# Half of the third modulation section, summed over its k-tiles by GpSimd during the first stage

## The chip, the core and the metric
One core of a Trainium2 chip runs the kernel. The metric is the device time of one execution in microseconds. Of the core's engines the text names TensorE (PE in the rows; PEld is its weight load), VectorE (DVE), ScalarE (ACT), GpSimd (POOL) and SyncE (SP). SP here only issues DMAs; its queue is "SP's queue".

## What is computed
One layer of a diffusion backbone on 128 context tokens and 256 latent tokens (three token tiles of 128) with D = 2048. What matters here is the modulation:

```python
mod_ctx = (silu(c_ctx) @ w_ada + b_ada)      # 6 * D columns: shift1, scale1, gate1, shift2, scale2, gate2
mod_lat = (silu(c) @ w_ada + b_ada)
h = rmsnorm(x, pre1) * (1.0 + scale1) + shift1
proj = h @ w_in                              # then DeltaNet heads (A), mLSTM heads (B)
x = x + gate1 * rmsnorm(mix @ w_out, post1)
h = rmsnorm(x, pre2) * (1.0 + scale2) + shift2
x = x + gate2 * rmsnorm(relu(h @ w1) ** 2 @ w2, post2)
```

`w_ada` has 2048 rows and 12288 columns of float32, so each of the six sections of 2048 columns is 16.8 MB. There are two condition vectors, one for context and one for latents. "The third modulation section", section 2 in the code, is gate1. It is needed only after the output projection.

## The kernel before
All weights are float32 and stream once from HBM. `gemm` (line 343) takes them in chunks of two k-tiles by 512 columns (512 KB). For each chunk `wchunk` (line 326) issues a load on SP's queue into one of five `raw` buffers, ScalarE casts it to a high part `whi`, VectorE subtracts to get the residual `wlo` (lines 338 and 339, both have two buffers), and TensorE makes three products per k-tile and tile (lines 362 to 368). So the chain load, cast, residual, product stands behind every chunk.

The stages are: stage 1 (`phase1`, line 393), which takes 9 pieces of k-tiles (1, 1, then 2 each) and for every piece runs 6 chunks: two for the mLSTM q and k, two for v, two for the output gate; in the last piece the gate columns follow (`gates`, line 523, a long list of small VectorE and TensorE instructions); then the mLSTM heads (`mlstm_head`, line 630), the DeltaNet quarters (lines 784 to 1057) with their own chunks, the output projection (`mid`, line 1082) and the FFN (line 1144).

The modulation is spread between the chunks. After every chunk `gemm` calls `fill` (line 241), which adds `S.rate` to a credit and takes that many steps from the list `S.todo`. A step is one turn of a generator. There are two kinds:

- `ada_steps` (line 177): TensorE multiplies the condition columns `c.scz` (128 rows, 32 columns of which two are used) with raw w_ada tiles, four column groups of 256 per k-tile side by side in one PSUM bank (line 196). The loads stand on SP's queue and use the same five `raw` buffers. At the end `ada_cols` (line 164) copies, transposes twice and copies back, and `ada_mod` adds the bias.
- `ada_vec` (line 210): VectorE multiplies a raw tile with a condition column and adds it to an accumulator (line 226); after 16 k-tiles TensorE sums over the partitions with a matrix of ones. It idles (yields) while its buffer `S.av` isn't there, which is until the output projection.

In stage 1 the list holds sections 0 and 1 at rate 2.0. After the mLSTM stage `body` (line 1222) appends the rest in this order: section 2 (two units of `ada_steps`, 16 k-tiles each), the gate rows, section 3, section 4, section 5, the last gate rows; rate 1.3 in the DeltaNet stage. `mid` drains the list up to the gate rows of gate1 first.

GpSimd in stage 1 issues a few small loads and selects at the start; later it takes the power in `rstd_of` (line 290), two kinds of small copies in the mLSTM heads (lines 635 and 683), and in the FFN a product (line 1163) and, at the very end, products with the gate rows (line 1183).

Each engine runs its instructions in one fixed order, made when the program is built: program order, but an instruction whose inputs come late may be overtaken by later ones, and parts marked with a high priority come early. Tiles are in pools; a tile with `bufs=1` can be taken again only when all that read the former one are done. When the pool of stage 1 (`S.p1`) closes, the mLSTM heads' tiles take its memory.

Of the kernel before, what the change touches and what calls it, by code (L numbers as in the profile page):

```python
# [12 lines left out]
F32 = mybir.dt.float32  # L13
F32R = mybir.dt.float32r
BF16 = mybir.dt.bfloat16
ALU = mybir.AluOpType
# [5 lines left out]
P = 128  # L22
D = 2048
NK = D // P
# [19 lines left out]

def setup(S):
    nc, tc, A = S.nc, S.tc, S.A
    cp, tp = S.cp, S.tp
    c = S.c = SimpleNamespace()

# [160 lines left out]
def ada_vec(S, sec, c0):  # L210

    nc, c = S.nc, S.c
    while S.av is None:
        yield
    acc = S.av.tile([P, 2, 512], F32, tag="adav", name="adav", bufs=1)
    for kt in range(NK):
        if kt % 2 == 0:
            raw = S.wp.tile([P, 2, 512], F32, tag="raw", name="raw_av", bufs=S.nraw)
            nc.sync.dma_start(raw, S.A.w_ada[0, kt * P:(kt + 2) * P, sec * D + c0:sec * D + c0 + 512]
                              .rearrange("(k p) n -> p k n", p=P))  # L220
        for v in range(2):
            w = c.scz[:, kt, v:v + 1]
            if kt == 0:
                nc.vector.tensor_scalar(acc[:, v, :], raw[:, 0, :], w, None, op0=ALU.mult)
            else:
                nc.vector.scalar_tensor_tensor(acc[:, v, :], in0=raw[:, kt % 2, :], scalar=w, in1=acc[:, v, :],  # L226
                                               op0=ALU.mult, op1=ALU.add)
        if kt % 2:
            yield
    ps = S.pa.tile([P, 512], F32, tag="a", name="ps_av")  # L230
    for j in range(4):
        nc.tensor.matmul(ps[32 * j:32 * j + 32, 0:256], lhsT=c.ones[:, 0:32], rhs=acc[:, j % 2, 256 * (j // 2):][:, 0:256],
                         start=True, stop=True)
    t = ada_cols(S, ps, 256)
    pv = S.wk.tile([P, 4, 2], F32, tag="modsum4", name="modsum4")
    for h in range(2):
        nc.vector.tensor_copy(pv[:, 2 * h:2 * h + 2, :].rearrange("p i v -> p v i"), t[:, 2 * h:2 * h + 2, :, 0])
    ada_mod(S, sec, c0 // P, 4, pv)


def fill(S, n=None):

    if n is None:
        S.credit += S.rate
        n = int(S.credit)
        S.credit -= n
    while n > 0 and S.todo:
        try:
            next(S.todo[0])
            n -= 1  # L250
        except StopIteration:
            S.todo.pop(0)
            n -= 1


def drain(S, left):
# [4 lines left out]
def ada_later(S, sec, nvec=0):  # L261

    for i in range(2):
        if i < 2 - nvec:
            S.todo.append(ada_steps(S, [(sec, 1024 * i + 256 * u) for u in range(4)], 256))
        else:
            S.todo.extend(ada_vec(S, sec, 1024 * i + 512 * h) for h in range(2))
# [75 lines left out]
def gemm(S, fm, wsrc, kcs, act, evac, psum=None, kn=2, between=None, room=()):  # L343

    nc = S.nc
    psum = psum or (lambda s: S.pg.tile([P, 512], F32, tag="g", name="ps_g"))
    ps = [None] * 4
    nl = len(kcs) - len(room)  # L350

    def products(s, i, kc, hi, lo):
        if ps[s] is None:
            ps[s] = psum(s)
        o = ps[s][:, 0:TOK] if fm else ps[s]
        w = slice(s * P, s * P + P)
        for kk in range(kn):
            ah, al = act(kn * kc + kk)
            st = i == 0 and kk == 0
            sp = i == len(kcs) - 1 and kk == kn - 1  # L360
            if fm:
                nc.tensor.matmul(o, lhsT=hi[:, kk, w], rhs=al, start=st, stop=False)  # L362
                nc.tensor.matmul(o, lhsT=hi[:, kk, w], rhs=ah, start=False, stop=False)  # L363
                nc.tensor.matmul(o, lhsT=lo[:, kk, w], rhs=ah, start=False, stop=sp)  # L364
            else:
                nc.tensor.matmul(o, lhsT=al[:, w], rhs=hi[:, kk, :], start=st, stop=False)  # L366
                nc.tensor.matmul(o, lhsT=ah[:, w], rhs=hi[:, kk, :], start=False, stop=False)  # L367
                nc.tensor.matmul(o, lhsT=ah[:, w], rhs=lo[:, kk, :], start=False, stop=sp)  # L368
    held = []
    for i, kc in enumerate(kcs):  # L370
        if between:
            between(i)
        w = wchunk(S, wsrc(kc), kn, room[i - nl] if i >= nl else None)
        ns = w[0].shape[2] // P if fm else NT
        if i >= nl:
            held.append((i, kc, *w))
            continue
        for s in range(ns):
            products(s, i, kc, *w)
            if i == len(kcs) - 1:  # L380
                evac(s, ps[s])
        fill(S)
    for s in range(ns if held else 0):
        for h in held:
            products(s, *h)
        evac(s, ps[s])
# [6 lines left out]
def phase1(S):  # L393

    nc, tc, A, c = S.nc, S.tc, S.A, S.c
# [6 lines left out]
    for t in range(NT):  # L402
        junk = p1.tile([P, D], F32, tag="junk", name="junk", bufs=1)
# [11 lines left out]
    for p, (k0, kn) in enumerate(pieces):  # L415
        if p == 0:
            drain(S, NP - 1)

        def acc(dst, src):
            if p == 0:  # L420
                nc.scalar.copy(dst, src)
            else:
                nc.vector.tensor_tensor(dst, src, dst, op=ALU.add)
        if p == 0:
            build_hT(S, xs, 0, 0, diag)
            for t in range(NT):
                nc.vector.tensor_scalar(xs[t], xs[t], r[:, t:t + 1], None, op0=ALU.mult)
            wgh, wgl = setup3(S, p1)

        def next_hT():  # L430
            if p < NP - 1:
                drain(S, NP - 2 - p)
                k1, n1 = pieces[p + 1]
                for kt in range(k1, k1 + n1):
                    build_hT(S, xs, kt, 0)
        kps = (k0 // kn,)
        ps = S.pm.tile([P, 512], F32, tag="m", name="ps_gates")
        for kk in range(kn):
            ah, al = S.hT(k0 + kk)
            for i, (w, a) in enumerate(((wgh, al), (wgh, ah), (wgl, ah))):  # L440
                nc.tensor.matmul(ps[0:GW, 0:TOK], lhsT=w[:, k0 + kk, :], rhs=a, start=kk == 0 and i == 0,
                                 stop=kk == kn - 1 and i == 2)
        acc(gT[0:GW, :], ps[0:GW, 0:TOK])
        for i, c0 in enumerate((C_BQ, C_BK)):
            gemm(S, True, wcols(w_in, c0, 512, kn), kps, S.hT, lambda s, ps, i=i: acc(S.bqk[s][:, i, :], ps[:, 0:TOK]),
                 kn=kn)
        for n in range(2):
            gemm(S, False, wcols(w_in, C_BV + 512 * n, 512, kn), kps, S.hT,
                 lambda s, ps, n=n: acc(S.vaug[s][:, 2 * n:2 * n + 2, 0:DVB],
                                        ps.rearrange("p (a b) -> p a b", a=2)), kn=kn)  # L450
        if p == NP - 1:
            for t in range(NT):
                nc.vector.memset(S.vaug[t][:, :, DVB:DVB + 1], 1.0)
            with tc.high_priority(HP):
                gates(S, gates_cols(S, gT))

        def bo_evac(s, ps, n):
            acc(bo[n][s], ps)
            if p == NP - 1:
                nc.scalar.activation(bo[n][s], bo[n][s], AF.Sigmoid)  # L460
                nc.sync.dma_start(S.gbd[s][:, n * 512:n * 512 + 512], bo[n][s])
        if p == 1:
            setup2(S)
        for n in range(2):
            if n == 1:
                next_hT()
            gemm(S, False, wcols(w_in, C_BO + 512 * n, 512, kn), kps, S.hT, lambda s, ps, n=n: bo_evac(s, ps, n),
                 kn=kn)
# [753 lines left out]
def body(tc, A, O):  # L1222
    with ExitStack() as ctx:
        nc = tc.nc
        S = SimpleNamespace(nc=nc, tc=tc, A=A, O=O, todo=[], credit=0.0, rate=1.7, nraw=5, av=None)
        ent = ctx.enter_context
        sub = lambda st, nm, bufs=1: st.enter_context(tc.tile_pool(name=nm, bufs=bufs, reuse_waits="tile"))
        S.cp = ent(tc.tile_pool(name="cp", bufs=1))
# [11 lines left out]
        with ExitStack() as mx:  # L1240
# [3 lines left out]
            with ExitStack() as ms:  # L1244
                S.mp = sub(ms, "mp")
                S.ga = sub(ms, "ga")
                with tc.tile_pool(name="p1", bufs=1, reuse_waits="tile") as S.p1:
                    with tc.tile_pool(name="tp", bufs=1, reuse_waits="tile") as S.tp:
                        setup(S)
                    phase1(S)  # L1250
                S.ml = sub(ms, "ml", 2)
                S.n1 = S.ml.tile([P, 8], F32, name="n1", bufs=1)
                for h in range(HB):
                    mlstm_head(S, h)
                mlstm_norms(S)
# [2 lines left out]
            S.de = sub(mx, "de", 2)  # L1258
            S.yA = S.da.tile([P, NT, 1024], F32, name="yA", bufs=1)
            delta_static(S)  # L1260
            ada_later(S, 2)
            S.todo.append(gate_step(S, 0))
            ada_later(S, 3)
            ada_later(S, 4, ND2)
# [43 lines left out]
```

## Time and profile before

| what | us |
|---|---|
| median of 3 runs (1989.87 to 1993.47) | 1989.95 |
| the profiled execution | 1993.48 |
| its span, first to last instruction | 1991.8 |
| TensorE busy | 1944.7 |
| VectorE busy | 1167.4 |
| ScalarE busy | 711.4 |
| GpSimd busy | 127.2 |

Times in the rows count from the start of the span. A group of the view by lines gives line, engine, operation, output and inputs, shapes and count; then the busy time, the mean of one in ns and the idle time before them with what ended it. A row of the timeline gives start, duration, engine, line, operation, tiles, shapes and count, and in brackets how long the engine had been idle and what ended that. "Releaser" and "waited for" are inferred from semaphores.

### The profile page before, as it was taken

The numbers are of one execution on the slowest core, as the hardware profiler recorded it, in microseconds if no ns is written. First come the engines' busy times: TensorE is split into PE (matmuls) and PEld (weight loads), VectorE is DVE, ScalarE is ACT, GpSimd is POOL, SyncE is SP. The second block draws the span as 40 slices with busy tenths as digits, with TensorE's granted clock in tenths as the row PEclk, the third lists the DMA queues.
The fourth block names the chain that finished last, engine by engine and source line by source line (L and its number), as shares of the span: only waits on it lengthen the run. The fifth ranks groups of instructions, "written<-read, shape, count | busy, mean of one in ns | idle before, by whom it ended". The sixth has DMA issues, their size and how long they took to land.

```text
span 1991.8 us, 28827 instructions
## 1 busy us (share of the span) xinstructions
PE 1944.7 (98%) x11334; PEld 1674.3 (84%) x11334; DVE 1167.4 (59%) x2146; ACT 711.4 (36%) x1125; POOL 127.2 (6%) x138
## 2 busy tenths in 40 slices
PE   6999999999999999998999999999999999999997
PEld 4777888888887777788998998988989989989886
DVE  3766885677877756767554565556543443343445
ACT  5222244644345324335433342332332423323322
POOL 3000000100000000000100010000000100000002
PEclk9999999999999999998999999999999999999999
DMA  8988436576656567762455555545544444444453
GB/s 274 299 263 267 124 113 213 177 219 167 184 168 174 167 183 222 265 190 75 148 159 158 169 159 155 161 154 165 158 138 127 127 128 127 129 130 126 133 170 106
DMA packets 229908, 337.25 MB, mean 169 GB/s; under 512 B 43808, under 2 KB 113136, under 8 KB 228748
## 3 DMA queue, kind: packets, MB, share of 16 engines
q1 hardware_dynamic: 211640, 333.14, 54.2%
q10 hardware_dynamic: 17620, 2.11, 0.7%
q8 instruction: 89, 1.46, 0.3%
q14 instruction: 47, 0.39, 0.1%
q0 software_dynamic: 512, 0.15, 0.1%
HBM read 326.80 MB, written 8.56 MB: 168 GB/s over the span
## 4 chain that ended last, share of the span: by engine, by line
PE 90%; DVE 4%; DMA 4%; ACT 1%; SPq 1%; issue 1%; POOL 0%; DVEq 0%; POOLq 0%; ACTq 0%
PE ps_g L362 13%; PE ps_g L364 12%; PE ps_g L363 12%; PE ps_dn L366 9%; PE ps_dn L368 8%; PE ps_dn L367 8%; PE ps_g L366 5%; PE ps_g L368 5%; PE ps_g L367 5%; PE ps_ada L196 4%; DMA raw<-w_in 2%; DVE wlo L339 1%; PE ps_num L694 1%; PE ps_o L1042 1%; PE ps_z L1008 1%
## 5 line engine op out<-in xcount | busy, mean ns | idle before, releaser
L339 DVE TENSOR_TENSOR wlo<-raw,whi 128x1024 fp32r<-128x1024 f32 (+1 forms) x402 | 487.5, 1213 | 558.0 <-ACT whi L338 556.9
L338 ACT CAST whi<-raw 128x1024 fp32r<-128x1024 f32 (+1 forms) x402 | 417.6, 1039 | 998.7 <-PE ps_g L363 386.8
L362 PE MATMUL ps_g<-h,whi 128*128 128x384 f32 x1536 | 522.7, 340 | 0.5 <-DVE cv L752 0.5
L364 PE MATMUL ps_g<-h,wlo 128*128 128x384 f32 x1536 | 516.5, 337 | 3.3 <-DVE wlo L339 3.3
L363 PE MATMUL ps_g<-h,whi 128*128 128x384 f32 x1536 | 516.7, 336 | 0.1
L362 PEld LDWEIGHTS ps_g<-h,whi 128*128 128x128 f32 x1536 | 288.9, 188 | 20.8 <-issue 18.4
L368 PE MATMUL ps_dn<-wlo,ah 128*128 128x512 f32 x756 | 294.5, 390 | 1.2 <-DVE wlo L339 1.2
L366 PE MATMUL ps_dn<-whi,al 128*128 128x512 f32 x756 | 294.9, 390 | 0.0
L367 PE MATMUL ps_dn<-whi,ah 128*128 128x512 f32 x756 | 294.5, 390 | 0.0
L364 PEld LDWEIGHTS ps_g<-h,wlo 128*128 128x128 f32 x1536 | 288.6, 188 | 6.6 <-DVE wlo L339 5.5
L363 PEld LDWEIGHTS ps_g<-h,whi 128*128 128x128 f32 x1536 | 289.0, 188 | 1.1 <-issue 0.7
L368 PEld LDWEIGHTS ps_dn<-wlo,ah 128*128 128x128 f32 x756 | 141.9, 188 | 31.6 <-DVE wlo L339 2.1
L366 PEld LDWEIGHTS ps_dn<-whi,al 128*128 128x128 f32 x756 | 141.9, 188 | 31.0 <-issue 1.6
L367 PEld LDWEIGHTS ps_dn<-whi,ah 128*128 128x128 f32 x756 | 141.9, 188 | 28.8
L226 DVE SCALAR_TENSOR_TENSOR adav<-raw_av,scz,adav 128x512 f32<-128x512 f32 x180 | 130.6, 774 | 13.2 <-DMA raw_av<-w_ada 13.1
L1163 POOL TENSOR_TENSOR rl<-rl 128x384 f32<-128x384 f32 x64 | 68.1, 1072 | 876.0 <-ACT ah L1162 875.9
L366 PE MATMUL ps_g<-whi,h 128*128 128x512 f32 x288 | 119.4, 415 | 0.6 <-ACT whi L338 0.6
L367 PE MATMUL ps_g<-whi,h 128*128 128x512 f32 x288 | 116.0, 403 | 0.0
L368 PE MATMUL ps_g<-wlo,h 128*128 128x512 f32 x288 | 114.4, 401 | 0.5 <-DVE wlo L339 0.5
L196 PE MATMUL ps_ada<-raw_ada,scz 128*32 128x256 f32 (+1 forms) x1216 | 101.7, 389 | 4.0 <-DMA raw_ada<-w_ada 2.6
L366 PEld LDWEIGHTS ps_g<-whi,h 128*128 128x128 f32 x288 | 54.8, 190 | 23.5 <-issue 11.5
L368 PE MATMUL ps_g<-wlo,y 128*128 128x512 f32 x180 | 71.1, 395 | 1.5 <-DVE wlo L339 1.5
(409 smaller groups left out, 1862.3 us busy)
## 6 DMA issues: line engine op xcount, KB each, us to landing
raw<-w_ffn SPq DMA_DIRECT2D x256, 512.0 KB, 3.8
raw_ada<-w_ada SPq DMA_DIRECT2D x80, 512.0 KB, 4.0
raw<-w_in SPq DMA_DIRECT2D x74, 512.0 KB, 4.0
raw_ada<-w_ada SPq DMA_DIRECT2D x128, 256.0 KB, 4.5
raw_av<-w_ada SPq DMA_DIRECT2D x48, 512.0 KB, 4.4
raw<-w_in SPq DMA_DIRECT2D x76, 256.0 KB, 3.9
raw<-w_out SPq DMA_DIRECT2D x32, 512.0 KB, 4.6
x<-x_sample SPq DMA_DIRECT2D x2, 1024.0 KB, 9.8
```

What stands on the lines that cost most here:

```text
L196: nc.tensor.matmul(ps[32 * j:32 * j + 32, 0:n], lhsT=c.scz[:, k + kk, :], rhs=raw[:, kk, u * n:u * n + n], start=k + kk < npar, stop=k + k ...
L226: nc.vector.scalar_tensor_tensor(acc[:, v, :], in0=raw[:, kt % 2, :], scalar=w, in1=acc[:, v, :], op0=ALU.mult, op1=ALU.add)
L338: nc.scalar.copy(hi, raw)
L339: nc.vector.tensor_tensor(lo, raw, hi.bitcast(F32), op=ALU.subtract)
L362: nc.tensor.matmul(o, lhsT=hi[:, kk, w], rhs=al, start=st, stop=False)
L363: nc.tensor.matmul(o, lhsT=hi[:, kk, w], rhs=ah, start=False, stop=False)
L364: nc.tensor.matmul(o, lhsT=lo[:, kk, w], rhs=ah, start=False, stop=sp)
L366: nc.tensor.matmul(o, lhsT=al[:, w], rhs=hi[:, kk, :], start=st, stop=False)
L367: nc.tensor.matmul(o, lhsT=ah[:, w], rhs=hi[:, kk, :], start=False, stop=False)
L368: nc.tensor.matmul(o, lhsT=ah[:, w], rhs=lo[:, kk, :], start=False, stop=sp)
L694: nc.tensor.matmul(o, lhsT=l, rhs=r, start=n == 0, stop=n == len(ops) - 1)
L1163: nc.gpsimd.tensor_tensor(rl, rl, rl, op=ALU.mult)
```

## The change
Columns 1024 to 2047 of section 2 leave the list after the mLSTM stage. Instead, from the third piece of stage 1 on, a second list `S.ptodo` holds two `ada_pool` generators for 512 columns each, called half 0 and half 1 in the text. Per step one pair of k-tiles is loaded by a DMA issued from GpSimd, one pair ahead, into a double buffer that takes the memory of an earlier scratch tile; GpSimd multiplies the raw tile with the condition column into `tmpp` and adds that to the accumulator `adap`, for each of the two conditions. `fill_pool` takes half a step per chunk. After 8 steps and two empty ones `ada_sum`, the tail of `ada_vec` made a function, sums over the partitions on TensorE and goes on as before. `adap`, the double buffer and `tmpp` have one buffer each. Steps left when stage 1 ends are taken right there.

```diff
--- before.py
+++ after.py
@@ -227,6 +227,43 @@
                                                op0=ALU.mult, op1=ALU.add)
         if kt % 2:
             yield
+    ada_sum(S, sec, c0, acc)
+
+
+def ada_pool(S, sec, c0):
+
+    nc, c = S.nc, S.c
+    acc = S.mp.tile([P, 2, 512], F32, tag="adap", name="adap", bufs=1)
+    both = S.p1.tile([P, 2, 2, 512], F32, tag="junk", name="rawp", bufs=1)
+
+    def load(kt):
+        raw = both[:, kt // 2 % 2]
+        nc.gpsimd.dma_start(raw, S.A.w_ada[0, kt * P:(kt + 2) * P, sec * D + c0:sec * D + c0 + 512]
+                            .rearrange("(k p) n -> p k n", p=P))
+        return raw
+    ahead = load(0)
+    for kt in range(0, NK, 2):
+        raw = ahead
+        if kt + 2 < NK:
+            ahead = load(kt + 2)
+        for kk in range(2):
+            for v in range(2):
+                w = c.scz[:, kt + kk, v:v + 1]
+                if kt + kk == 0:
+                    nc.gpsimd.tensor_scalar(acc[:, v, :], raw[:, 0, :], w, None, op0=ALU.mult)
+                else:
+                    tmp = S.p1.tile([P, 512], F32, tag="tmpp", name="tmpp", bufs=1)
+                    nc.gpsimd.tensor_scalar(tmp, raw[:, kk, :], w, None, op0=ALU.mult)
+                    nc.gpsimd.tensor_tensor(acc[:, v, :], acc[:, v, :], tmp, op=ALU.add)
+        yield
+    for _ in range(2):
+        yield
+    ada_sum(S, sec, c0, acc)
+
+
+def ada_sum(S, sec, c0, acc):
+
+    nc, c = S.nc, S.c
     ps = S.pa.tile([P, 512], F32, tag="a", name="ps_av")
     for j in range(4):
         nc.tensor.matmul(ps[32 * j:32 * j + 32, 0:256], lhsT=c.ones[:, 0:32], rhs=acc[:, j % 2, 256 * (j // 2):][:, 0:256],
@@ -251,6 +288,16 @@
         except StopIteration:
             S.todo.pop(0)
             n -= 1
+
+
+def fill_pool(S):
+    S.pcredit += S.prate
+    while S.pcredit >= 1 and S.ptodo:
+        S.pcredit -= 1
+        try:
+            next(S.ptodo[0])
+        except StopIteration:
+            S.ptodo.pop(0)
 
 
 def drain(S, left):
@@ -380,6 +427,7 @@
             if i == len(kcs) - 1:
                 evac(s, ps[s])
         fill(S)
+        fill_pool(S)
     for s in range(ns if held else 0):
         for h in held:
             products(s, *h)
@@ -461,6 +509,9 @@
                 nc.sync.dma_start(S.gbd[s][:, n * 512:n * 512 + 512], bo[n][s])
         if p == 1:
             setup2(S)
+        if p == 2:
+            S.ptodo = [ada_pool(S, 2, 1024 + 512 * h) for h in range(2)]
+            S.prate = 0.5
         for n in range(2):
             if n == 1:
                 next_hT()
@@ -1222,7 +1273,7 @@
 def body(tc, A, O):
     with ExitStack() as ctx:
         nc = tc.nc
-        S = SimpleNamespace(nc=nc, tc=tc, A=A, O=O, todo=[], credit=0.0, rate=1.7, nraw=5, av=None)
+        S = SimpleNamespace(nc=nc, tc=tc, A=A, O=O, todo=[], credit=0.0, rate=1.7, nraw=5, av=None, pcredit=0.0, prate=0.0, ptodo=[])
         ent = ctx.enter_context
         sub = lambda st, nm, bufs=1: st.enter_context(tc.tile_pool(name=nm, bufs=bufs, reuse_waits="tile"))
         S.cp = ent(tc.tile_pool(name="cp", bufs=1))
@@ -1248,6 +1299,9 @@
                     with tc.tile_pool(name="tp", bufs=1, reuse_waits="tile") as S.tp:
                         setup(S)
                     phase1(S)
+                while S.ptodo:
+                    S.prate = 1.0
+                    fill_pool(S)
                 S.ml = sub(ms, "ml", 2)
                 S.n1 = S.ml.tile([P, 8], F32, name="n1", bufs=1)
                 for h in range(HB):
@@ -1258,7 +1312,7 @@
             S.de = sub(mx, "de", 2)
             S.yA = S.da.tile([P, NT, 1024], F32, name="yA", bufs=1)
             delta_static(S)
-            ada_later(S, 2)
+            S.todo.append(ada_steps(S, [(2, 256 * u) for u in range(4)], 256))
             S.todo.append(gate_step(S, 0))
             ada_later(S, 3)
             ada_later(S, 4, ND2)
```

## Rows read from the trace of the kernel before
**Rows 1.** The page: head, GpSimd's busy tenths in 40 slices, chain of waits by engine.
```profile
span 1991.8 us, 28827 instructions
...
POOL 3000000100000000000100010000000100000002
...
PE 90%; DVE 4%; DMA 4%; ACT 1%; SPq 1%; issue 1%; POOL 0%; DVEq 0%; POOLq 0%; ACTq 0%
```

**Rows 2.** Busy times of stretches of stage 1; columns in the first row.
```profile
core 0: us, PE busy (x) PEld busy (x) DVE busy (x) ACT busy (x) POOL busy (x), PEclk, DMA share, GB/s
...
40.00:80.00 40.00, 39.43 (x277) 26.02 (x279) 27.13 (x61) 14.97 (x26) 0.00 (x0) 1.00 0.97 315
80.00:120.00 40.00, 39.93 (x271) 29.98 (x270) 25.62 (x41) 8.09 (x9) 0.00 (x0) 1.00 0.84 263
...
200.00:260.00 60.00, 60.00 (x301) 52.80 (x300) 50.36 (x78) 17.73 (x20) 0.31 (x2) 1.00 0.43 124
260.00:300.00 40.00, 39.67 (x205) 33.53 (x204) 30.65 (x87) 17.75 (x25) 0.00 (x0) 0.96 0.36 111
```

**Rows 3.** Waits, 25 to 200 us: total, times, longest.
```profile
ACT whi L338 <- DMA raw<-w_in: 67.8, 21, 5.9
```

**Rows 4.** Timeline at 118 us: start, us, engine, line, out<-in, count [idle before].
```profile
118.04 1.04 ACT L338 CAST whi<-raw 128x1024 fp32r<-128x1024 f32 x1 [5.33 <-DMA raw<-w_in]
...
120.40 0.50 PE L368 MATMUL ps_g<-wlo,h 128*128 128x512 f32 x1 [0.47 <-DVE wlo L339]
```

**Rows 5.** Timeline at 221 us: VectorE, then TensorE.
```profile
220.74 1.23 DVE L339 TENSOR_TENSOR wlo<-raw,whi 128x1024 fp32r<-128x1024 f32 x1 [0.17 <-ACT whi L338]
...
224.22 0.39 PE L368 MATMUL ps_g<-wlo,h 128*128 128x512 f32 x1
```

**Rows 6.** Groups by line, TensorE, 300 to 800 us.
```profile
L196 PE MATMUL ps_ada<-raw_ada,scz 128*32 128x256 f32 x638 | 59.7, 389 | 0.0
```

**Rows 7.** Timeline at 409 us, TensorE.
```profile
409.19 1.07 PE L196 MATMUL ps_ada<-raw_ada,scz 128*32 128x256 f32 x16
```

**Rows 8.** Line 1183 on GpSimd: min/median/max in ns.
```profile
L1183 POOL TENSOR_TENSOR y<-y,gp x9: 1288/1298/2280, 1931.6 to 1966.7; 128x512 f32<-128x512 f32 x9
```

**Rows 9.** Groups by line and shape, GpSimd, whole span.
```profile
L129 POOL DMA_DIRECT2D gbias<-mlstm_ibias x1 | 1.5, 1504 | 0.0
L764 POOL MEMSET Tm<- 128x768 f32 x2 | 1.4, 741 | 0.0
```

**Rows 10.** Timeline at 1965 us, VectorE.
```profile
1964.75 0.69 DVE L1177 TENSOR_TENSOR y<-ps_dn,y 128x512 f32<-128x512 f32 x1 [0.67 <-PE ps_dn L368]
1965.82 2.01 DVE L339 TENSOR_TENSOR wlo<-raw,whi 128x1024 fp32r<-128x1024 f32 x1 [0.38 <-ACT whi L338]
```

**Rows 11.** Timeline of the same stretch, GpSimd.
```profile
1964.19 4.78 POOL L1183 TENSOR_TENSOR y<-y,gp 128x512 f32<-128x512 f32 x3 [11.55 <-ACT fj L1180]
```

**Rows 12.** Chain of waits in order of time, 200 to 260 us.
```profile
201.57 0.66 PE ps_hT L303 x6
...
228.01 0.66 PE ps_hT L303 x6
```

**Rows 13.** Timeline, VectorE, the gate columns: first, one between, last.
```profile
263.90 0.20 DVE L531 TENSOR_TENSOR gz<-gt,gbias 128x48 f32<-128x48 f32 x1
...
270.19 0.20 DVE L555 SCALAR_TENSOR_TENSOR gg<-gl,gea 128x48 f32<-128x48 f32 x1
...
295.25 0.17 DVE L511 TENSOR_TENSOR r3r<-r3r,nmrp 128x24 f32<-128x24 f32 x1
```

**Rows 14.** Timeline at 270 us, TensorE.
```profile
270.90 1.40 PE L564 MATMUL ps_cum<-gg,tri 128*128 128x8 f32 x12
```

**Rows 15.** Chain of waits in order of time, 255 to 312 us: stage 1's last product.
```profile
294.37 0.23 PE ps_g L368
```

**Rows 16.** Timeline, GpSimd, 255 to 312 us.
```profile
254.94 0.31 POOL L635 COPY cn<-n 128x2 f32<-128x2 f32 x2 [233.26 <-PE ps_hT L303]
311.35 0.19 POOL L683 COPY n<-cf 128x1 f32<-128x1 f32 x1 [56.10 <-ACT cf L681]
```

## The prediction
> **What bounds the kernel now.** I read the page's chain of waits first: 90% of the span is TensorE work [rows 1], so a microsecond counts where TensorE has to wait or is spared instructions. Next the busy times by stretch of stage 1, where the change puts its work [rows 2]. Three regimes are to be seen. From 40 to 80 us the DMA engines are 0.97 busy at 315 GB/s. From 80 to 120 us they are 0.84 busy at 263 and TensorE is full. From 200 to 260 us, the first two modulation sections being through, DMA moves 124 GB/s and TensorE alone sets the pace. Then ScalarE's wait list: the cast of each weight chunk waits 67.8 us in all for its load between 25 and 200 us [rows 3]. Chunks come just in time: at 118 us the cast had waited 5.33 us for a load, and TensorE then waited 0.47 us for the residual that VectorE makes of it [rows 4]. After 200 us there is room: the residual that ends at 221.97 is first used at 224.22 [rows 5]. GpSimd does nothing from 40 to 120 us and 0.31 us from 200 to 260 [rows 2].
>
> **What is taken away.** One unit of section 2 goes: 16 k-tiles by 4 column groups, each in two passes, so 128 TensorE records. Between 300 and 800 us 638 such records took 59.7 us, 94 ns each [rows 6], which gives 12.0 us; sixteen back to back took 1.07 us [rows 7], which gives 8.6 us. I take the middle, 10.3 us, all of it on TensorE's path. Its 16 loads leave SP's queue in a stretch where other waits end later, so I count nothing for them, and no loss if that is wrong. Added are two final sums, each 8 records of the same form (0.6 us) with a pair of transposes of about 0.2 us each, while one pair goes: 1.6 us. **Net gain 8.7 us.** The drains further on are the same: of the list one unit is missing, so later units come some 16 steps sooner and the column-wise ones wait, idle, for their buffer until the output projection.
>
> **GpSimd's work.** Per pair of k-tiles there are 4 products with a column scalar, 4 additions (2 fewer in the first pair) and one load issue. An addition of two 128x512 tiles takes 1.30 us (median of nine) [rows 8]. No row shows the product, which reads one tile and writes one. Below, a memset only writes: 0.74 us at 768 columns [rows 9], 0.49 for 512 in proportion; above, the addition's 1.30. I take 0.65, nearer the memset, since one stream is read where the addition reads two. A load issue took up to 1.50 us [rows 9] and at the least nothing; I take 1.0. A pair then costs 5.2 + 2.6 + 1.0 = 8.8 us, eight pairs 70 us. The Trainium skill (GPSIMD Engine Reference, 3.1 Elementwise — side-by-side cycle accounting) measures 769 ns for 512 elements of the best one-input loop; by that price, an estimate, each half would take 4 us more and the sum would be 4 us worse.
>
> **The two engines exclude each other.** Beside a run of GpSimd additions, a VectorE addition that reads PSUM kept its 0.69 us while the residual, with two operands in SBUF, took 2.01 us instead of 1.23 [rows 5, 10]; the three GpSimd additions together took 4.78 us instead of 3.9 [rows 11]. They run by turns. Each residual thus costs GpSimd up to 1.1 us and may itself wait for what is left of a GpSimd instruction: half of a mean of 1.0 us. Six chunks take 26.4 us without the modulation beside them [rows 12], so there is a residual every 4.4 us or, before 200 us, somewhat more; a pair takes about 11 us.
>
> **Where that work falls.** Half 0 has no one to wait for but GpSimd's own setup, which is over within the first of the page's slices of 50 us [rows 1]; I have it start at 22 us, whatever the half-step pacing in the program says, and end at 110. Half 1 writes the accumulator that TensorE's final sum of half 0 must first have read. That sum stands behind the 22nd of 38 chunks. The transposes for the next piece, one chunk from the end of a piece, are at 201.57 and 228.01 [rows 12]; the sum, two chunks into the piece between, at about 215 before any shift. So half 1 runs from about 220 to 310.
>
> - **A, loads in half 0.** 0.52 MB per 11 us is 48 GB/s. At 40 to 80 us there is room for 10 (315/0.97 = 325) [rows 2]: 38 GB/s short for 40 us is 1.5 MB or 4.7 us. From 80 us the room, 50 GB/s (263/0.84 = 313), suffices. I take 4 us, bounds 0 and 9 (all but none of the room usable). The Trainium skill (DMA: Bandwidth & Descriptors, Measured (HBM→SBUF, 128 partitions, SWDGE, issued from GpSimd)) gives 425 GB/s for large transfers; by that ceiling A would be zero and the sum 4 us better. None of the stretches in the rows passes 315.
> - **B, residuals in half 0.** About 19 chunks by 0.45 us is 8.5 us of lateness. Where a chunk has no room [rows 4] it is TensorE's, elsewhere it is hidden; I take a third, 3 us, bounds 0 and 8.
> - **C, the gates.** Half 1 meets a residual with 2.2 us of room [rows 5], so nothing until 262. Then VectorE works through the gate columns, 28 instructions with two SBUF operands from 263.90 to 295.25 [rows 13], it is busy 30.65 of 40 us [rows 2], and TensorE's cumulative sums start at 270.90, half a microsecond behind their operand [rows 13, 14]. 28 by 0.45 us is 12.6; over half of it reaches TensorE, which takes its instructions in order: 7 us, bounds 0 and 15. The granted clock is 0.96 of full there already [rows 2]; what a further drop would cost is inside the 15.
> - **D, the end of half 1.** Half 1's final sum stands at the end of stage 1, whose last product is at 294.37 [rows 15]; with A, B and C, 308. GpSimd ends at about 312. TensorE waits 4 us there, bounds 0 and 20; behind the GpSimd work also stand the first copy and the state copies of the mLSTM heads, now at 254.94 and 311.35 [rows 16], and the latter is just in time. The heads' tiles take the memory that stage 1 gives back, GpSimd's load buffer included; if a load of SP's queue lands there, it and every weight load behind it wait for GpSimd too, which is in the upper bound.
>
> **Sum:** -8.7 + 4 + 3 + 7 + 4 = +9.3 us on the profiled execution's 1993.5 (a span of 1991.8 [rows 1] and 1.7 around it). The median of the runs shown, 1989.95, lies 3.5 lower; on it the forecast is 1999 us.
>
> **Rivals.**
> - **The cover holds (faster).** A to D come to 3 us: loads slip into gaps, lateness is absorbed. Then 1990 - 8.7 + 3 = 1984 us. For it: from 40 to 120 us TensorE lost only 0.6 us of 80 [rows 2] although its chunks come just in time. Against: a chunk without room is already there [rows 4], and the turns of the two engines are plain [rows 10, 11].
> - **The sum of half 0 is pulled forward (even).** If the order of TensorE's instructions puts it soon after 110 us, half 1 runs from 110 to 205, where DMA room like that of 80 to 120 us [rows 2] just holds it. C and D go, some 2 us of lateness come in the like of B: -8.7 + 4 + 3 + 2 = 0, 1990 us. Against: the transposes above stand where the program has them.
> - **GpSimd late (much slower).** With the product at its upper bound, 1.30, a pair takes 11.4 us and 14 with the turns; half 1 would end at 335, and TensorE, held at the final sum, would wait 27 us: 1990 + 5.3 + 27 = 2022. It decides as soon as a pair takes over 11 us.
> - **It doesn't do what it says.** If half 1 doesn't overlap stage 1 at all, the end is that of the last rival, and it is counted there.
>
> **Numbers.** Forecast (1994 to 2010) 0.40, cover 0.25, even 0.20, GpSimd late 0.15. About 0.2% (4 us) is what a measurement of this kernel can tell from no change; so faster 0.25, same 0.20, slower 0.55. The range goes from 1982, most of the cover case, to 2022, half of the late one.
>
> **What would show it.** Right: half 0 on GpSimd from about 22 us, a gap, half 1 from about 220; residuals of up to 2.5 us beside it; DMA share about 1.0 from 40 to 80 us; TensorE waiting for gate columns at 262 to 300 and for the accumulator at the final sum; 128 fewer records of the column form later and TensorE 9 us shorter there. Wrong: half 1 before 200 us (even), residuals of 1.23 us beside busy GpSimd (C and B gone), stage 1 ending within 2 us of before (faster), or products far from 0.65 us.

## The result and the profile after

The changed kernel takes 2037.82 us (median of 4 runs, 2037.23 to 2042.19) against 1990.04 for the kernel before on the same chip: a ratio of 1.0236, 95% interval 1.022 to 1.0251. It is 48 us slower; the forecast was 9 us slower, the range went up to 2022. Lines of the changed kernel have numbers 47 to 51 higher from `gemm` on (the cast is L385, the residual L386, the products L409 to L415); in the runs with further edits they are one or two higher again.

The page of the changed kernel: head, GpSimd's busy tenths and the granted clock in 40 slices, chain of waits by engine, to be read beside [rows 1].

```profile
span 2040.5 us, 28749 instructions
...
POOL 7960495001000000000011000010000000100002
PEclk9999985999999999999999999999999999999999
...
PE 84%; POOL 5%; DVE 5%; DMA 4%; issue 1%; ACT 1%; SPq 0%; DVEq 0%; POOLq 0%; ACTq 0%
```

Slices are 51 us here. GpSimd now works in the first three, rests in the fourth, and works on to the seventh. In the seventh slice TensorE was granted half its clock, and GpSimd, 0% of the chain before, has 5% of it, some 100 us. The stretches of [rows 2], with two more behind them (PE, PEld, DVE, ACT, POOL busy, granted clock, DMA share, GB/s):

```profile
40.00:80.00 40.00, 33.61 (x237) 20.78 (x234) 25.41 (x52) 12.21 (x23) 38.06 (x27) 1.00 0.92 299
80.00:120.00 40.00, 38.26 (x241) 27.71 (x241) 29.63 (x48) 8.35 (x10) 38.02 (x26) 1.00 0.90 296
200.00:260.00 60.00, 59.97 (x328) 50.09 (x326) 49.49 (x83) 16.26 (x19) 28.06 (x18) 1.00 0.57 177
260.00:300.00 40.00, 24.81 (x125) 21.34 (x123) 28.36 (x51) 10.68 (x13) 38.16 (x26) 0.88 0.40 120
300.00:332.00 32.00, 0.00 (x0) 0.00 (x0) 0.00 (x0) 0.00 (x0) 30.15 (x23) 0.50 0.09 31
332.00:350.00 18.00, 17.30 (x59) 14.45 (x60) 4.27 (x16) 1.65 (x4) 3.74 (x5) 0.55 0.01 2
```

Two separate losses are to be seen. From 40 to 120 us TensorE is busy 71.9 of 80 us instead of 79.4, while GpSimd is busy nearly all the time. And from 300 to 332 us TensorE, VectorE and ScalarE do nothing at all; GpSimd alone works. TensorE's timeline says what that was (start, us, engine, line, tiles, shapes, count, idle time before and its releaser):

```profile
284.52 0.34 PE L411 MATMUL ps_g<-h,wlo 128*128 128x384 f32 x1
332.70 1.06 PE L269 MATMUL ps_av<-adap,ones 128*32 128x256 f32 x2 [47.84 <-POOL adap L257]
...
336.42 1.93 PE L615 MATMUL ps_cum<-gg,tri 128*128 128x8 f32 x9
```

TensorE waited 47.84 us for the accumulator `adap` with the first product of half 1's final sum, and the gates' cumulative sums (L615, at 270.90 before [rows 14]) stood close behind it. GpSimd's groups over the span by line and shape (L256 is the product, L257 the addition, L253 the first products of a half; busy us, mean ns, idle before and releaser) give the pace of the work waited for, and its timeline a stretch in which no other engine moves gives the undisturbed prices:

```profile
L256 POOL TENSOR_SCALAR tmpp<-rawp,scz 128x512 f32<-128x512 f32 x60 | 105.8, 1763 | 10.0 <-DMA rawp<-w_ada 4.9
L257 POOL TENSOR_TENSOR adap<-adap,tmpp 128x512 f32<-128x512 f32 x60 | 82.1, 1369 | 4.9
...
L253 POOL TENSOR_SCALAR adap<-rawp,scz 128x512 f32<-128x512 f32 x4 | 7.6, 1904 | 92.5 <-PE ps_av L269 89.2 <-DMA rawp<-w_ada 3.2
```

```profile
306.68 1.26 POOL L257 TENSOR_TENSOR adap<-adap,tmpp 128x512 f32<-128x512 f32 x1
308.04 1.56 POOL L256 TENSOR_SCALAR tmpp<-rawp,scz 128x512 f32<-128x512 f32 x1
309.69 1.26 POOL L257 TENSOR_TENSOR adap<-adap,tmpp 128x512 f32<-128x512 f32 x1
310.89 0.76 POOL L241 DMA_DIRECT2D rawp<-w_ada  x1
```

A product with a column scalar takes 1.56 us by itself, more than the addition of two tensors (1.26). From product to product it is 3.0 us, so an undisturbed pair of k-tiles takes 4 x 3.0 and 0.8 for the load's issue: 12.8 us. Half 0 took 13.4 us a pair (26.3 to 133.7). L253 shows the rest of the delay: half 1 stood 89.2 us until TensorE had read half 0's sums at 230.

**Where the 48.7 us of span come from.** Four instructions that both kernels have make a ledger. Their rows in the view by tile (count: shortest, median, longest ns, first to last start), first of before, then of after: the transposes of stage 1 (`ps_hT<-ident,x`, the last is for the last piece), the heads' state products (`ps_cn`), and the transposes of the second norm (`ps_hT<-ident,xr`).

```profile
L303 PE MATMUL ps_hT<-ident,x x45: 271/273/330, 46.5 to 254.8; 128*128 128x128 f32 x45
L303 PE MATMUL ps_hT<-ident,xr x36: 270/271/273, 913.6 to 931.3; 128*128 128x128 f32 x36
```
```profile
L679 PE MATMUL ps_cn<-vaug,ks x16: 377/379/484, 310.3 to 385.2; 128*128 128x257 f32 x16
```
```profile
L350 PE MATMUL ps_hT<-ident,x x45: 270/273/329, 49.8 to 270.3; 128*128 128x128 f32 x45
L350 PE MATMUL ps_hT<-ident,xr x36: 270/271/273, 963.3 to 981.0; 128*128 128x128 f32 x36
```
```profile
L730 PE MATMUL ps_cn<-vaug,ks x16: 377/380/484, 379.5 to 453.5; 128*128 128x257 f32 x16
```

The last transposes of stage 1 are 15.5 us late (254.8 to 270.3), the cumulative sums 65.5 (270.9 to 336.4), the last state product 68.3, the second norm 49.7, the end 48.7. So: lateness of stage 1 +15.5, the hold +50.0, behind it +2.8 (the clock is still at 0.55 up to 350 us), the DeltaNet stage and the output projection -18.6, the rest -1.0.

### The profile page after: what moved, and what is told of

Its sections match the earlier page's. It is cut to its first block, busy times and chain, and to the rows that moved or that the text cites. A ratio compares the mean times of both kernels' runs of the same rounds, so it can differ in the third digit from the quotient of the medians.

```text
span 2040.5 us, 28749 instructions
## 1 busy us (share of the span) xinstructions
PE 1937.2 (95%) x11224; PEld 1674.3 (82%) x11224; DVE 1180.9 (58%) x2153; ACT 711.4 (35%) x1126; POOL 333.1 (16%) x278
## 4 chain that ended last, share of the span: by engine, by line
PE 84%; POOL 5%; DVE 5%; DMA 4%; issue 1%; ACT 1%; SPq 0%; DVEq 0%; POOLq 0%; ACTq 0%
PE ps_g L409 13%; PE ps_g L411 13%; PE ps_g L410 12%; PE ps_dn L415 8%; PE ps_dn L413 8%; PE ps_dn L414 8%; PE ps_g L413 4%; PE ps_g L415 4%; PE ps_g L414 4%; PE ps_ada L196 3%; POOL tmpp L256 2%; DVE wlo L386 2%; POOL adap L257 2%; DMA raw<-w_in 1%; DMA raw_ada<-w_ada 1%
## 5 line engine op out<-in xcount | busy, mean ns | idle before, releaser
L386 DVE TENSOR_TENSOR wlo<-raw,whi 128x1024 fp32r<-128x1024 f32 (+1 forms) x402 | 492.7, 1226 | 563.8 <-ACT whi L385 563.2
L385 ACT CAST whi<-raw 128x1024 fp32r<-128x1024 f32 (+1 forms) x402 | 417.6, 1039 | 998.4 <-PE ps_g L410 395.1
L409 PE MATMUL ps_g<-h,whi 128*128 128x384 f32 x1536 | 522.8, 340 | 0.5 <-ACT whi L385 0.5
L409 PEld LDWEIGHTS ps_g<-h,whi 128*128 128x128 f32 x1536 | 288.5, 188 | 21.9 <-issue 18.1
L415 PE MATMUL ps_dn<-wlo,ah 128*128 128x512 f32 x756 | 294.6, 390 | 0.9 <-DVE wlo L386 0.9
L415 PEld LDWEIGHTS ps_dn<-wlo,ah 128*128 128x128 f32 x756 | 141.9, 188 | 31.3 <-DVE wlo L386 2.0
L415 PE MATMUL ps_g<-wlo,h 128*128 128x512 f32 x288 | 116.3, 407 | 3.0 <-DVE wlo L386 2.9
L256 POOL TENSOR_SCALAR tmpp<-rawp,scz 128x512 f32<-128x512 f32 x60 | 105.8, 1763 | 10.0 <-DMA rawp<-w_ada 4.9
L196 PE MATMUL ps_ada<-raw_ada,scz 128*32 128x256 f32 (+1 forms) x1088 | 87.7, 388 | 9.6 <-DMA raw_ada<-w_ada 8.3
L257 POOL TENSOR_TENSOR adap<-adap,tmpp 128x512 f32<-128x512 f32 x60 | 82.1, 1369 | 4.9
```

Source lines behind the costliest of these rows:

```text
L196: nc.tensor.matmul(ps[32 * j:32 * j + 32, 0:n], lhsT=c.scz[:, k + kk, :], rhs=raw[:, kk, u * n:u * n + n], start=k + kk < npar, stop=k + k ...
L256: nc.gpsimd.tensor_scalar(tmp, raw[:, kk, :], w, None, op0=ALU.mult)
L257: nc.gpsimd.tensor_tensor(acc[:, v, :], acc[:, v, :], tmp, op=ALU.add)
L385: nc.scalar.copy(hi, raw)
L386: nc.vector.tensor_tensor(lo, raw, hi.bitcast(F32), op=ALU.subtract)
```

## The experiments

The table gives the same ledger for every run, in us against the profiled kernel before, each from the rows of that view. "Stage 1" is the last transposes for its last piece, "sums" the gates' first cumulative sum, "heads" the last state product, "norm" the second norm's first transposes. In c4 and d1 TensorE's fixed order has the gates 40 instructions later, so their "sums" stand for themselves. A ledger is of one execution each, and executions of one kernel differ: twelve of d1 lie between 1977.9 and 1988.8 us, and the profiled executions lie from 3.2 us below the median of their kernel (b2) to 4.4 above it (the changed kernel; before: 3.4 above). So differences of 2 or 3 us in a row of the table show little.

| run | median | ratio to before | stage 1 | sums | heads | norm |
|---|---|---|---|---|---|---|
| the changed kernel | 2037.8 | 1.022 to 1.0251 | +15.5 | +65.5 | +68.3 | +49.7 |
| b1 product as two-input | 2031.8 | 1.0183 to 1.023 | +20.6 | +55.4 | +58.1 | +39.7 |
| b2 no loads | 2033.7 | 1.0192 to 1.025 | +8.5 | +56.2 | +55.2 | +38.2 |
| b3 half 0 only | 1991.9 | 0.9988 to 1.0021 | +12.5 | +12.5 | +12.9 | -1.3 |
| b4 sum behind heads | 2010.0 | 1.0076 to 1.0126 | +13.5 | +17.3 | +33.1 | +17.3 |
| c1 half 1 early | 1990.1 | 0.9988 to 1.0013 | +13.9 | +15.9 | +14.7 | -3.2 |
| c2 early, two-input | 1999.5 | 1.0027 to 1.0056 | +25.6 | +25.8 | +23.0 | +5.9 |
| c3 one half from 180 | 1996.3 | 1.0017 to 1.0038 | +6.6 | +12.0 | +16.1 | +4.6 |
| c4 one half from 150 | 1989.7 | 0.9985 to 1.001 | +14.5 | +21.9 | +12.5 | +0.3 |
| d1 column scalar from 150 | 1984.3 | 0.9953 to 0.9976 | +7.4 | +14.8 | +4.1 | -11.0 |
| d2 column scalar from 180 | 1995.9 | 1.0013 to 1.0037 | +4.8 | +8.2 | +11.9 | +3.8 |

**Only half 0 on GpSimd.** What do the two losses cost apart?

```diff
-            S.ptodo = [ada_pool(S, 2, 1024 + 512 * h) for h in range(2)]
+            S.ptodo = [ada_pool(S, 2, 1024)]
...
+            S.todo.append(ada_steps(S, [(2, 1536 + 128 * u) for u in range(4)], 128))
             S.todo.append(gate_step(S, 0))
```

> Edit: half 1 isn't given to GpSimd; its 512 columns go back to TensorE as one list unit of four groups of 128 columns. Theory H (the final sum of half 1 holds TensorE for 48 us): the lateness of 15.5 us before the gates stays, the hold and the later 4 us vanish, and of the 20 us won later about half remains: 1990 + 15.5 - 10 = 1995 us, 1990 to 2001. Rival S (stage 1 is slowed by GpSimd's loads and turns as a whole, and half 0 carries half of the loss): about 2014.

1991.9 us, ratio 1.0004: no difference that can be measured, and inside what theory H expected. The lateness of stage 1 is there (12.5 us), the hold is gone, and 14.2 us come back later. The 46 us between this kernel and the changed one are thus half 1's.

**The final sum behind the heads.** Was it GpSimd's pace alone, or the place of the sum in TensorE's order?

```diff
-                while S.ptodo:
-                    S.prate = 1.0
-                    fill_pool(S)
...
                     mlstm_head(S, h)
+                while S.ptodo:
+                    S.prate = 1.0
+                    fill_pool(S)
                 mlstm_norms(S)
```

The sum also takes its PSUM buffer from the heads' pool, so that it isn't pulled ahead again. TensorE's order differs from the changed kernel's in a few other places too.

> Edit: the final sum of half 1 stands behind the mLSTM heads in the program, with a PSUM buffer of the heads' kind so that it isn't taken earlier; GpSimd's work is as in the changed kernel. Theory H with the place (the first of its four products stands ahead of the gates' cumulative sums and some 24 us of stage 1's products): TensorE goes on at 284.5 and runs some 24 us further. If nothing else waits for GpSimd, the hold vanishes and the kernel takes about 1990 us (2037.8 - 48). If the first copies of the heads on GpSimd, or heads' tiles in the memory of GpSimd's load buffer, wait for the end of half 1 at 335, a hold of about 25 us remains: 2012 us. Rival (GpSimd's own backlog is what the stage needs, the place of the sum doesn't matter): 2034 to 2040.

2010.0 us: 28 of the 48 us were the place, and the time is that of the expectation with a remaining hold (2012), though not as one wait of 25 us. The cumulative sums are 17.3 us late instead of 65.5. What is still lost, 15.8 us between them and the last head, shows in TensorE's waits from 285 to 425 us and in a wait of SP's queue in the same stretch (engine, tile, line, what it waited for, us in total, times, longest):

```profile
PE ps_num L746 <- POOL cn L687: 6.8, 1, 6.8
PE ps_cn L731 <- DVE ks L729: 3.3, 1, 3.3
PE ps_g L414 <- DVE gl L600: 2.7, 1, 2.7
...
SPq L763 <- POOL tmpp L256: 14.4, 1, 14.4
```

The first of these is the heads' copy on GpSimd, which stands behind the last addition of half 1 and runs at 338.35 (254.94 before [rows 16]). The last line is a load for the first head (`gb`). By its releaser it takes memory of `tmpp`, so it had to wait for GpSimd's last products: SP's queue issued nothing from 322.5 to 337.1 us, and the next weight chunk reached ScalarE at 346.4. TensorE's 3.3 us at 351.4 stand at the end of that chain (chunk, cast, residual, `ks`), when GpSimd was done. This is the case that the forecast has in D's upper bound. So the waiting for GpSimd was not gone with the place of the sum; part of it moved to the copy and to SP's queue. How the 15.8 us divide between the two isn't shown.

**Half 1 early.** The other way to be rid of the hold: half 1 starts sooner, because TensorE reads half 0's accumulator sooner.

```diff
-    for _ in range(2):
+    for _ in range(2 if c0 == 1024 else 19):
         yield
...
-            S.prate = 0.5
+            S.prate = 1.0
```

The early sum takes its PSUM buffer from the pool of the transposes, since the other one is held by an unfinished unit of sections 0 and 1 at that time.

> Edit: a whole GpSimd step per chunk instead of half a step, so that the final sum of half 0 stands behind the 11th chunk instead of the 22nd; 19 empty steps instead of 2 keep the sum of half 1 where it was; the early sum takes a PSUM buffer of another pool. Theory H (half 1 came late because it waited 89 us for TensorE's sum of half 0): half 1 runs from about 145 to 255, in the stretch where SP's loads are still dense, so the lateness before the gates grows from 15.5 to about 20 us, but the hold of 48 us and the gates' delay are gone: 1990 + 20 - 20 (the gain measured later) = 1990 us, 1986 to 1996. Rival T (the early sum is itself reached by TensorE before GpSimd is through half 0, and the wait only moves): 2005 or more.

1990.1 us, ratio 1.0001. GpSimd ran half 1 from 169 to 283 us, TensorE never waited for `adap`, and the 48 us are gone. The lateness grew less than expected: 13.9 instead of 20. Why the second half costs 1 or 2 us when it follows a first, and a half by itself 5 or more (below), stays open.

**The loads.** What part of the lateness of stage 1 is theirs?

```diff
-            ahead = load(kt + 2)
+            ahead = load(kt + 2) if kt == 0 else both[:, (kt // 2 + 1) % 2]
```

> Edit: each half loads its first two pairs of k-tiles only and computes all eight passes on these two buffers, so 12 of the 16 GpSimd loads (6.3 MB) are left out; the arithmetic is unchanged. Part of the computation changed: 12 of 16 k-tiles of these columns are replaced by others. In the changed kernel the transposes for the last piece (before: 254.8) come 15.5 us late. Theory A (loads compete with SP's queue): that lateness falls to 3 us or less and the kernel takes about 2026. Theory B (turns of VectorE and GpSimd): it stays at 12 or more and the kernel stays at 2034 to 2038. As recorded in the forecast, A 4 and B 3 of 7, about half each: 8 us late. The hold at the final sum stays, 45 us or more, under all of them, since a pair only loses its load issue (0.8 us) and its rare waits.

8.5 us late at the last transposes instead of 15.5: 7.0 us went with the 12 loads. The 8.5 that stay I put down to the turns; four loads are left in them, and no run leaves out the turns alone. Four profiles with the same half 0 lie between 12.5 and 15.5, so each part is good to some 2 us. The hold stayed (45.4 us), as all theories had it.

**The price of the product.** The same product as an operation of two tensors, the condition column repeated along the row:

```diff
-                    nc.gpsimd.tensor_scalar(tmp, raw[:, kk, :], w, None, op0=ALU.mult)
+                    nc.gpsimd.tensor_tensor(tmp, raw[:, kk, :], w.to_broadcast([P, 512]), op=ALU.mult)
```

> Edit: GpSimd's product is written as an operation of two tensors, the second operand being the condition column repeated along the row, instead of tensor and column scalar (1.56 us undisturbed in the changed kernel). Theory P (the price of the product sets the loss): if this form costs the 1.27 us of GpSimd's addition, a pair is 4 x 0.29 = 1.2 us shorter, eight pairs 9.3 us; half 1 ends near 325 instead of 335 and the kernel takes about 2028 us. If it costs 1.56 or more, 2038 or above. Rival L (the loads set GpSimd's pace, not its arithmetic): the product gets shorter but the pairs stay at 13 us, 2038 us.

GpSimd's groups from 300 us to the end of half 1, with nothing beside it:

```profile
L257 POOL TENSOR_TENSOR adap<-adap,tmpp 128x512 f32<-128x512 f32 x9 | 11.3, 1261 | 0.7
L256 POOL TENSOR_TENSOR tmpp<-rawp,scz 128x512 f32<-128x512 f32 x9 | 9.4, 1040 | 0.6
```

1.04 us: a third less than with the column scalar. Half 1 ended at 325, as expected, TensorE waited 32.8 us instead of 47.8, and yet only 6 of these 15 us show: stage 1 became 5 us later (20.6). The run with half 1 early and this product repeats that.

> Edit: as the run with half 1 early, and the product as an operation of two tensors (1.04 us instead of 1.56). Theory H: GpSimd is done sooner, but does the same number of turns and loads in a shorter time, so the lateness before the gates is 20 us or a little more, as it grew from 15.5 to 20.6 with that product alone: 1988 to 1998 us. Rival (a faster product lowers the lateness, since VectorE waits for less): 1980 to 1986.

1999.5 us, above the expected range and 9 us above the same kernel with the slower product. TensorE, VectorE, ScalarE and GpSimd run the same instructions in the same order in both profiles, but for the form of the product. So a shorter GpSimd instruction made the kernel slower, and the two forms must differ in what they do to the other engines.

**One half, later.** Two runs with the two-input product asked whether the lateness belongs to the dense stretch before 200 us. A copy of one column, taken from a tile that VectorE writes in the piece of that time, holds GpSimd back; the sum follows the heads or, where its turn in the list still comes in stage 1 (c4 and d1 below), stands in the last piece.

```diff
+    nc.gpsimd.tensor_copy(acc[:, 0, 0:1], S.bqk[1][:, 1, 0:1])
     ahead = load(0)
...
-        if p == 2:
+        if p == 5:
```

> Edit: only one half goes to GpSimd, with the product of two tensors, and it starts when VectorE has written the mLSTM q and k of the sixth piece (about 185 us); its final sum stands behind the mLSTM heads; the other 512 columns are TensorE's as in the run with half 0 alone. Theory S (the lateness comes from the stretch before 200 us, where loads are dense and chunks have no room): about 2 us before the gates and 2 in the gates are lost, and the 14 us that half 0 alone gained later are kept: 1990 - 14 + 4 = 1980 us, 1976 to 1985. Rival U (a half costs 12 us of lateness wherever it runs): 1988 to 1992.

> Edit: as the run before, started with the fifth piece (about 152 us). Theory S: half of its 88 us lie in the dense stretch, so 5 to 6 us of lateness, no time in the gates: 1990 - 14 + 6 = 1982 us, 1978 to 1987. Rival U (a half costs 12 us of lateness wherever it runs): 1988 to 1992.

1996.3 and 1989.7 us: theory S is wrong in both, and the first is above rival U as well. From 150 us on a half costs 14.5 us of lateness; from 180 on 6.6 and another 9.5 through the gates, where the granted clock fell to 0.77 between 270 and 290 us (0.91 before).

**The form of the product.** In five profiles with the column scalar (the changed kernel, b4, c1, d1, d2), counted from their timelines, 57 residuals of 1024 columns start while such a product runs: 13 of them take over 1.3 us, the others 1.21 to 1.3 as they do alone. Of 42 that start while an addition runs, 30 take over 1.3 us. In the four profiles with the two-input product (b1, c2, c3, c4) 20 of 30 that start while the product runs do. VectorE and then GpSimd in a stretch of the run d1 (below), where the residual is L388, the product L257 and the addition L258:

```profile
214.63 2.08 DVE L388 TENSOR_TENSOR wlo<-raw,whi 128x1024 fp32r<-128x1024 f32 x1
...
232.19 1.22 DVE L388 TENSOR_TENSOR wlo<-raw,whi 128x1024 fp32r<-128x1024 f32 x1 [0.17 <-ACT whi L387]
```

```profile
214.34 1.30 POOL L258 TENSOR_TENSOR adap<-adap,tmpp 128x512 f32<-128x512 f32 x1
...
216.38 1.77 POOL L257 TENSOR_SCALAR tmpp<-rawp,scz 128x512 f32<-128x512 f32 x1
...
231.23 1.58 POOL L257 TENSOR_SCALAR tmpp<-rawp,scz 128x512 f32<-128x512 f32 x1
232.89 1.67 POOL L258 TENSOR_TENSOR adap<-adap,tmpp 128x512 f32<-128x512 f32 x1
```

The residual at 214.63 starts during an addition, waits for its end at 215.64 and takes 2.08 us. The one at 232.19 starts during a product with a column scalar (231.23 to 232.81) and keeps 1.22 us; the addition behind it waits for the residual (1.67 us). With two-input products most residuals wait in either case, and more than residuals are hit. VectorE in the run c4:

```profile
176.87 1.63 DVE L359 TENSOR_TENSOR h<-hfull,h 128x384 fp32r<-128x384 f32 x1
...
183.54 2.72 DVE L388 TENSOR_TENSOR wlo<-raw,whi 128x1024 fp32r<-128x1024 f32 x1
186.18 1.24 DVE L155 TENSOR_TENSOR adatmp<-modsum,pcol 128x4 f32<-128x4 f32 x1
```

The high and low parts of the next transposes (L359, 0.55 us before), and even a column operation of 4 elements (L155, 0.15 before), wait a microsecond or more. So the last two runs take the kernels of c4 and c3 with the column scalar:

> Edit: one half on GpSimd from the fifth piece on, its sum behind the heads, the other 512 columns TensorE's, as in the run of one half from 150, but with the product of tensor and column scalar again (1.56 us) instead of two tensors (1.04 us). Theory M (VectorE takes turns only with GpSimd's instructions of two tensors: a residual that starts while one runs takes 1.7 to 1.9 us, while a product with a column scalar runs 1.25 to 1.31): the lateness before the gates falls from 14.5 to some 5 us, as half 1 in the run of half 1 early cost 2.7 us there, and the 12 to 14 us gained later stay: 1990 - 13 + 5 = 1982 us, 1978 to 1986. Rival U (a half costs 12 us of lateness whatever its form): 1988 to 1992. Rival W (the slower product makes it worse, as more GpSimd time meets VectorE): 1993 or more.

> Edit: as the run before, started with the sixth piece (about 190 us); GpSimd ends at about 300 instead of 283. Theory M: 2 to 4 us before the gates instead of 6.5, and the gates, which lost another 9.5 with two tensors, lose 4 as in the run with the sum behind the heads; the first copies of the heads wait little: 1990 - 12 + 7 = 1985 us, 1980 to 1990. Rival (the gate columns are the place where the turns cost most, and they meet more of GpSimd's time now): 1996 or more.

The run from 150 takes 1984.3 us, ratio 0.9965 (0.9953 to 0.9976), as theory M expected: 5 us better than with two-input products, and faster than both kernels. The lateness of stage 1 is 7.4 instead of 14.5. It isn't that fewer loads fall there: from 170 to 210 us the DMA engines moved 270 and 279 GB/s, 249 and 263 in c4. Nor is it the order: up to the end of the heads each engine's order in d1 is that of c4, and in d2 that of c3.

The run from 180 takes 1995.9 us and misses theory M's range (1980 to 1990); it is no better than its twin c3. GpSimd works on to 300 us, through the gates, and 7.1 us are lost between the last transposes and the heads (4.8 to 11.9). But its twin loses 9.5 there and is 4 us later behind the heads; by the second norm that lead is gone (3.8 and 4.6), and no run shows why. Against d1, TensorE has the gates at another place in its order, so what the later start costs by the gates' turns and what by the order isn't told apart.

So in all four pairs (b1 and the changed kernel, c2 and c1, c4 and d1, c3 and d2) stage 1 is later with the two-input product, by 5.1, 11.7, 7.1 and 1.8 us. The kernel's time is longer by it in two of them, 9 and 5 us; in b1 GpSimd's earlier end outweighs it, and c3 and d2 take the same time.

## Why the prediction was wrong

The direction was right, the size not, and the measured time lies 16 us above the range.

**The step that failed first** is the price of the product: "I take 0.65, nearer the memset, since one stream is read where the addition reads two". It is 1.56 us, above even the upper bound of 1.30. The bound rested on the thought that an operation that reads less can't take longer than the addition; the row that would have been needed, a product with a column scalar on GpSimd, was nowhere in the trace, and no reason excluded a higher price. The Trainium skill (GPSIMD Engine Reference, 3.1 Elementwise — side-by-side cycle accounting) has 769 ns for 512 elements of the best one-input loop; the trace shows twice that for this form. The rival "GpSimd late" had the mechanism, the point from which it decides (a pair over 11 us) and the end of half 1 (335; the sum's products started at 332.7). It was given 0.15 and 2022 us. That its 335 agrees is partly chance: it came from a lower price (1.30), an earlier start (220, measured 230.85) and a longer pair (14 us, measured 13.1).

**The step that failed second** lifts 2022 to 2038: the final sum was put "at the end of stage 1", its program place. In TensorE's fixed order its first product stands just ahead of the cumulative sums, which began at 270.90 while the last product of stage 1 came at 294.37 [rows 14, 15]. So some 23 us of products that could have hidden the wait stood behind it; the run with the sum behind the heads gave back 28 us. That an instruction whose inputs come late may be overtaken was known (The kernel before); that the sum may be pulled ahead into a gap was thought of for half 0 alone, in the even rival.

- **A, the loads:** 4 forecast (0 to 9), 7.0 measured, by the 12 loads left out in b2. The sign that the forecast gave, a DMA share of about 1.0 from 40 to 80 us, is 0.92 at 299 GB/s in the changed kernel and 0.97 at 322 in b3, with the same half 0. How the loads make stage 1 late isn't shown.
- **B, the turns in half 0:** 3 forecast (0 to 8), 8.5 measured, as what stays without the 12 loads. Two things were missing: the h parts and the column operations wait too, and not only residuals; and products with a column scalar let the residuals pass, which made it less than it would have been (b1).
- **C, the gates:** 7 forecast. 3.8 in the run with the sum behind the heads (13.5 to 17.3), 2.0 with half 1 early; in the changed kernel the hold covers it.
- **D, the end of half 1:** 4 forecast (0 to 20), 50 measured; without the place of the sum still 16, with 6.8 of waiting for the heads' copy and a load on SP's queue held for 14.4; the forecast had named both, the second for GpSimd's load buffer.
- **The gain:** 8.7 forecast, 18.6 measured between the heads and the second norm. There it is to be held against the 10.3 for the records, as the two final sums (1.6) stand ahead of that stretch. The groups of L196 in that stretch, of before (385.2 to 913.6 us) and of after (453.5 to 963.3):

```profile
L196 PE MATMUL ps_ada<-raw_ada,scz 128*32 128x256 f32 x528 | 48.3, 389 | 0.0
```
```profile
L196 PE MATMUL ps_ada<-raw_ada,scz 128*32 128x256 f32 x400 | 36.2, 388 | 0.0
```

The 128 records took 12.1 us, 95 ns each, as in [rows 6]; the mean with the back-to-back price of [rows 7] was a mistake, since the records stand among others. The other 6.5 us are 4 of TensorE's other busy time and 2.4 of its waits; no run asked for their cause.

**The even rival** (half 0's sum pulled forward, 1990 us) was built as the run with half 1 early and gave 1990.1. That its sum came out is partly chance: lateness and gain were each 5 to 9 us larger than it had them.

## What to carry to other kernels

Work given to an idle engine costs through the engines it shares turns with and through the first instruction that waits for its result; look that instruction up in the consumer's order, with the work behind it, before anything else. Where no row shows an operation of the new engine, there is no safe upper bound for it, so ask at which price the plan breaks and give that case its chance. And choose among equal operations by what they do to the neighbour: here the slower form of the product made the faster kernel.

## What the runs showed of the hardware

- On GpSimd a 128x512 float32 product with a column scalar takes 1.56 us, the same product as an operation of two tensors with the column repeated 1.04, the addition of two full tensors 1.26 to 1.30. One input was the dearest.
- A VectorE residual, with two SBUF operands, that began during a GpSimd two-input instruction took over 1.3 us (alone 1.21 to 1.3) in 30 of 42 cases for the addition and 20 of 30 for the product. During a product with a column scalar it did in 13 of 57; that product waited when it came second (2.42 us in the median of 59, against 1.56). The Trainium skill (SBUF — State Buffer, Who interferes with whom) has the two exclude each other whenever GpSimd's instruction reads SBUF, whichever starts first keeping the other out. For two-input instructions the traces agree in most cases; for the column scalar only in one order.
- TensorE's granted clock is 0.50, the level of 1.2 GHz, from 300 to 332 us, after it had waited since 284.9, and its first products behind the hold ran at that level: a product of 512 columns took 0.63 us instead of 0.39.
